# The feed-forward layers of two token chunks by Strassen's algorithm: seven block products in place of eight

## The chip, the cores and the metric

One core of a Trainium2 chip runs the whole program. The engines are TensorE (PE in the rows, its weight load PEld), VectorE (DVE), ScalarE (ACT), GpSimd (POOL) and SyncE (SP), which only issues transfers here. The metric is the device time of one execution in microseconds (us); the time before is 3068.78 us, the median of three runs (3066.46 to 3073.22).

## What is computed

One layer of a decoder: a projection, three groups of heads (mLSTM, RWKV-7, differential attention), an output projection with a residual, and a feed-forward layer with a residual; then a final norm. SEQ is 2048, D_MODEL 1024, D_FF 4096, all in float32. What the change touches is the end:

```
x = x + concat(A, B, C) @ w_out
x = x + relu(RMSNorm(x) @ w_ff_up)^2 @ w_ff_down
out = RMSNorm(x) * final_g
```

## The kernel before

The sequence is cut in four chunks of T = 512 tokens, features on the 128 partitions. After the heads, class `Tail` handles a chunk: `load` brings the mixed heads of the chunk in from DRAM and splits each of 8 tiles into a high and a low part, `outproj` multiplies by w_out and adds the residual (tiles `x2`, 8 per chunk), `hidden` is the norm and splits the result (`hh`, `hl`), `ffn` is the feed-forward layer, `final` the last norm and the store.

Every float32 product is made of three matmuls (`mm3`): high by high, high by low, low by high, each of a 128x128 weight tile against 512 tokens. `Weights.get` loads a unit of weights in four parts and splits each: ACT writes the high part `whi`, POOL subtracts for the low part `wlo` (lines 174 and 175, `split`). There are six buffers each of `whi` and `wlo`.

Chunks 0 and 1 go through `ffn` one after the other; chunks 2 and 3 go through it together (two `items`), so each unit of weights serves both: 16 steps `fb`, in each `up(fb)` with 96 matmuls and `down(fb)` with 96, for the two chunks. `down` adds its product to `x2` in place, on DVE (line 1176). Chunk 2 has a set of pools of its own (`tr`), chunk 3 has those of `tl`; the tile `nacc`, in which `norm` sums the squares and then keeps the scale that it multiplies by, is there once in each set.

The text order around chunk 3 is: with step 16 of chunk 1's `ffn` come `outproj(3)` and `hidden(x3)`, then the last `down` of chunk 1, then the `ffn` of chunks 2 and 3, and within its first step `final(1, x1)`. The order in each engine's queue is made from the text by a list scheduler, which takes priorities from the text order (`high_priority` puts a block first); where two tiles share a buffer, the one that is first in the text has it first.

Of the kernel before, what the change touches and what calls it, by code (L numbers as in the profile page):

```python
# [40 lines left out]
def load(nc, i, out, in_):  # L41
    (nc.sync if i % 2 == 0 else nc.scalar).dma_start(out, in_)
# [6 lines left out]
class Lane:  # L49


    def __init__(s, tc, p):
        s.tc, s.p = tc, p
# [91 lines left out]
    nc.tensor.matmul(ps, e.ones, dg, start=True, stop=True)  # L145


def norm(tc, e, sp, raw, pp, ptag, src, gofs, emit, w=T):
# [20 lines left out]
    for k in range(KT):  # L169
# [49 lines left out]
class Proj:  # L219
# [855 lines left out]
class Tail:  # L1075


    def __init__(s, ctx, tc, e, xt, wo, wu, wd, out, nh, nx, nr=3, w=None):
        s.tc, s.e, s.xt, s.wo, s.wu, s.wd, s.out = tc, e, xt, wo, wu, wd, out
        p = lambda n, **k: ctx.enter_context(tc.tile_pool(name=n, **k))  # L1080
        s.nr = nr
        s.hp = p("th", bufs=nh)
        s.xp = p("tx", bufs=nx)
        s.w = w or Weights(tc, e, p("tw", bufs=2))
        s.ap = p("ta", bufs=2)
        s.np = p("tn", bufs=2)
        s.pd = p("pdt", bufs=2, space=PSUM)
        s.py = p("pyt", bufs=2, space=PSUM)

    def hl(s):  # L1090
        return (s.hp.tile([P, T], F32R, name="hh", tag="hh"), s.hp.tile([P, T], F32R, name="hl", tag="hl"))

    def raw(s):
        return s.np.tile([P, T], F32, name="traw", tag="traw", bufs=s.nr)

    def load(s, c):

        nc = s.tc.nc
        m = []
        for k in range(KT):  # L1100
            r = s.raw()
            load(nc, k, r, s.e.mixT[c][k * P:(k + 1) * P])
            t = s.hl()
            split(nc, t[0], t[1], r, nc.vector)
            m.append(t)
        return m

    def outproj(s, c, m, x2, xp):
        nc = s.tc.nc
        for u in range(4):  # L1110
            w = s.w.get(s.wo[u], 256)
            for j in range(2):
                d = 2 * u + j
                xr = s.raw()
                load(nc, d, xr, s.xt[c, d])
                ps = s.pd.tile([P, T], F32, name="pd", tag="pd")
                mm3(nc, ps, [(*w(k, j * P, (j + 1) * P), m[k][0], m[k][1]) for k in range(KT)])
                t = xp.tile([P, T], F32, name="x2", tag="x2")
                with s.tc.high_priority():
                    nc.vector.tensor_tensor(t, ps, xr, ALU.add)  # L1120
                x2.append(t)
            yield u

# [13 lines left out]
            norm(s.tc, s.e, s.np, s.raw, s.pd, "pd", x2, V_N2, emit)  # L1137
        return h2

    def ffn(s, items):  # L1140

        tc, nc = s.tc, s.tc.nc
        FB = 16
        acts = {}

        def up(fb):
            w = s.w.get(s.wu[fb], 256)
            acts[fb] = []
            for tl, x2, h2 in items:
                ah = tl.ap.tile([P, 2, T], F32R, name="ah", tag="ah")  # L1150
                al = tl.ap.tile([P, 2, T], F32R, name="al", tag="al")
                for j in range(2):
                    ps = tl.pd.tile([P, T], F32, name="pd", tag="pd")
                    mm3(nc, ps, [(*w(k, j * P, (j + 1) * P), h2[k][0], h2[k][1]) for k in range(KT)])
                    with tc.high_priority():
                        r = tl.raw()
                        nc.scalar.activation(r, ps, AF.Relu)
                        nc.scalar.activation(r, r, AF.Square)
                        split(nc, ah[:, j], al[:, j], r, nc.vector)
                acts[fb].append((ah, al))  # L1160

        def down(fb):
            w = s.w.get(s.wd[fb], 1024, kt=2)
            av = acts.pop(fb)
            last = fb == FB - 1
            parts = [(d, i) for d in range(KT) for i in range(len(items))]
            if last:

                parts.sort(key=lambda x: x[1])
            for d, i in parts:  # L1170
                tl, x2, h2 = items[i]
                ah, al = av[i]
                ps = (s if last else tl).py.tile([P, T], F32, name="py", tag="py")
                mm3(nc, ps, [(*w(j, d * P, (d + 1) * P), ah[:, j], al[:, j]) for j in range(2)])
                with tc.high_priority():
                    nc.vector.tensor_tensor(x2[d], ps, x2[d], ALU.add)  # L1176

        up(0)
        yield 0
        for fb in range(1, FB):  # L1180
            up(fb)
            yield fb
            down(fb - 1)
        yield FB
        down(FB - 1)
# [14 lines left out]
            norm(s.tc, s.e, s.np, s.raw, s.pd, "pd", x2, V_FG, emit)  # L1200


@with_exitstack
def tile_hybrid_layer(ctx: ExitStack, tc: tile.TileContext, xt, wi, wg, wm, wo, wu, wd, vf, vg, lw, hb, tb, lq, cm, out, dbg=None, upto=9):
    nc = tc.nc
    e = Env()
# [4 lines left out]
    def scr(name, shape):  # L1211
        return e.dp.tile(shape, F32, name=name)
# [40 lines left out]
    xs = {}  # L1253
# [45 lines left out]
    if upto < 3:  # L1299
        actx.close()  # L1300
        return
    tl = Tail(ctx, tc, e, xt, wo, wu, wd, out, nh=10, nx=17)
    x0, x1, x2, x3 = [], [], [], []
    for _ in tl.outproj(0, tl.load(0), x0, tl.xp):
        pass
    h0 = tl.hidden(x0)
    for fb in tl.ffn([(tl, x0, h0)]):
        if fb == 15:
            m1 = tl.load(1)
        if fb == 16:  # L1310
# [90 lines left out]
```

## Time and profile before

| | us |
|---|---|
| median of three runs | 3068.78 |
| the profiled execution's own time | 3073.17 |
| its span in the trace | 3071.4 |
| feed-forward of chunks 2 and 3, last `down` of chunk 1 ahead of it, to the last matmul | about 2315 to 3045 |
| from the last such matmul to the end | about 26 |

The profiled execution is 4.4 us above the median. A row of the stage view gives for a stretch how long each engine was busy, how many instructions it ran (x), and the granted TensorE clock (PEclk: 1.00 is 2.4 GHz, 0.50 is 1.2 GHz). A matmul's own duration in the rows is longer than its turn, since matmuls overlap: the turn is read from how many run in a stretch. In the timeline a row's bracket says how long its engine was idle before it and what ended that.

### The profile page before, as it was taken

What the parts mean: (1) busy time and instruction counts of PE and PEld (TensorE: products, weight loads), DVE (VectorE), ACT (ScalarE), POOL (GpSimd) and SP (SyncE); (2) the same over time, 40 slices, a digit from 0 to 9 for tenths busy, and PEclk for the clock granted to TensorE, in tenths of its full rate; (3) what the DMA queues carried; (4) which work ended last, traced back from release to release, by engine and by line L of the source; (5) the groups of instructions that cost most, each with busy time, mean ns of one, the idle gap of its engine ahead of it and who ended that gap; (6) DMA issues with size and microseconds to landing.
All of it is one profiled execution on the core that took longest, in us unless ns stands there. A gap on an engine that the chain in (4) does not pass through costs nothing.

```text
span 3071.4 us, 47398 instructions
## 1 busy us (share of the span) xinstructions
PE 2959.1 (96%) x17232; PEld 2431.0 (79%) x17232; DVE 1719.6 (56%) x4055; ACT 1201.4 (39%) x2389; POOL 1090.1 (35%) x1047
## 2 busy tenths in 40 slices
PE   9999999999999889999999999999999999999997
PEld 7886787778878767888888788888787888888885
DVE  6587878677773456554555765554365333333335
ACT  5343334223322445544545555444344223222323
POOL 4354444333433214433333433433454222222223
PEclk9999999999999889999999999999999999999998
DMA  8445333643543554444446343332452111111111
GB/s 307 128 135 198 88 92 84 214 117 92 149 150 115 158 147 109 110 121 109 115 107 170 101 128 104 109 103 76 131 154 81 53 49 48 42 54 50 48 42 66
DMA packets 285348, 342.03 MB, mean 111 GB/s; under 512 B 99349, under 2 KB 161078, under 8 KB 284090
## 3 DMA queue, kind: packets, MB, share of 16 engines
q1 hardware_dynamic: 203914, 233.46, 26.3%
q10 hardware_dynamic: 81200, 105.53, 12.1%
q8 instruction: 136, 2.23, 0.3%
q14 instruction: 98, 0.80, 0.1%
HBM read 264.68 MB, written 74.21 MB: 110 GB/s over the span
## 4 chain that ended last, share of the span: by engine, by line
PE 63%; DMA 3%; DVE 2%; POOL 1%; SPq 1%; ACT 0%; issue 0%; DVEq 0%; ACTq 0%; POOLq 0%
PE pd L182 10%; PE pd L183 10%; PE pd L184 10%; PE py L182 8%; PE py L183 7%; PE py L184 7%; PE pO L1056 4%; PE pS L1026 2%; PE pS L1027 2%; PE pT L1051 2%; DMA Qd<-aql 1%; DMA traw<-mixT 0%; POOL x L1194 0%; PE nps L145 0%; DMA Qd<-aqh 0%
## 5 line engine op out<-in xcount | busy, mean ns | idle before, releaser
L175 POOL TENSOR_TENSOR wlo<-wraw,whi 128x512 fp32r<-128x512 f32 (+2 forms) x560 | 765.7, 1380 | 1322.9 <-ACT whi L174 885.1
L174 ACT ACTIVATE whi<-wraw 128x512 fp32r<-128x512 f32 (+2 forms) x560 | 347.1, 626 | 660.8 <-PE py L183 370.6
L1176 DVE TENSOR_TENSOR x<-py,x 128x512 f32<-128x512 f32 x512 | 350.1, 689 | 443.0 <-PE py L184 440.6
L182 PE MATMUL pd<-hh,whi 128*128 128x512 f32 x1280 | 504.3, 397 | 4.3 <-ACT hh L174 4.3
L183 PE MATMUL pd<-hl,whi 128*128 128x512 f32 x1280 | 504.4, 395 | 1.1 <-DVE hl L175 1.1
L184 PE MATMUL pd<-hh,wlo 128*128 128x512 f32 x1280 | 501.5, 395 | 0.0
L182 PE MATMUL py<-ah,whi 128*128 128x512 f32 x1024 | 405.0, 398 | 0.7 <-ACT whi L174 0.5
L183 PE MATMUL py<-al,whi 128*128 128x512 f32 x1024 | 400.4, 394 | 0.6 <-DVE al L175 0.6
L184 PE MATMUL py<-ah,wlo 128*128 128x512 f32 x1024 | 399.0, 394 | 1.2 <-POOL wlo L175 1.2
L182 PEld LDWEIGHTS pd<-hh,whi 128*128 128x128 f32 x1280 | 241.5, 189 | 58.1 <-ACT hh L174 5.6
L183 PEld LDWEIGHTS pd<-hl,whi 128*128 128x128 f32 x1280 | 242.0, 189 | 55.1 <-DVE hl L175 2.5
L184 PEld LDWEIGHTS pd<-hh,wlo 128*128 128x128 f32 x1280 | 241.8, 189 | 52.5 <-issue 0.2
L1030 DVE TENSOR_SCALAR_CACHE_REDUCE E<-pS 128x512 f32<-128x512 f32 (+4 forms) x320 | 185.9, 607 | 152.2 <-PE pS L1027 95.3
L175 DVE TENSOR_TENSOR al<-traw,ah 128x512 fp32r<-128x512 f32 x128 | 113.6, 888 | 215.8 <-ACT ah L174 215.1
L182 PE MATMUL pd<-hhi,whi 128*128 128x512 f32 x544 | 224.5, 416 | 7.6 <-ACT hhi L279 6.5
L184 PEld LDWEIGHTS py<-ah,wlo 128*128 128x128 f32 x1024 | 192.2, 188 | 44.7 <-POOL wlo L175 1.6
L182 PEld LDWEIGHTS py<-ah,whi 128*128 128x128 f32 x1024 | 192.6, 188 | 43.4 <-ACT whi L174 1.1
L183 PEld LDWEIGHTS py<-al,whi 128*128 128x128 f32 x1024 | 192.5, 188 | 42.4 <-DVE al L175 0.8
L184 PE MATMUL pd<-hhi,wlo 128*128 128x512 f32 x544 | 225.4, 417 | 0.0
L183 PE MATMUL pd<-hlo,whi 128*128 128x512 f32 x544 | 224.3, 414 | 0.4 <-POOL hlo L175 0.3
L1037 ACT ACTIVATE E<-E,nm 128x128 f32<-128x128 f32 (+15 forms) x128 | 153.7, 1201 | 99.2 <-DVE nm L1033 81.9
L182 PE MATMUL pd<-whi,hhi 128*128 128x256 f32 (+1 forms) x640 | 188.5, 295 | 2.5 <-DVE evx L408 1.2
(370 smaller groups left out, 5105.1 us busy)
## 6 DMA issues: line engine op xcount, KB each, us to landing
wraw<-in_wu ACTq DMA_DIRECT2D x96, 256.0 KB, 3.2
wraw<-in_wu SPq DMA_DIRECT2D x96, 256.0 KB, 3.2
wraw<-in_wd ACTq DMA_DIRECT2D x96, 256.0 KB, 3.2
wraw<-in_wd SPq DMA_DIRECT2D x96, 256.0 KB, 3.1
wraw<-in_wi ACTq DMA_DIRECT2D x48, 256.0 KB, 3.6
wraw<-in_wi SPq DMA_DIRECT2D x48, 256.0 KB, 3.6
feat<-hhi SPq DMA_DIRECT2D x4, 2048.0 KB, 9.5
feat<-hlo SPq DMA_DIRECT2D x4, 2048.0 KB, 12.4
```

What stands on the lines that cost most here:

```text
L174: nc.scalar.activation(hi, src, AF.Copy)
L175: lo_eng.tensor_tensor(lo, src, hi.bitcast(F32), ALU.subtract)
L182: nc.tensor.matmul(out, sh, mh, start=(i == 0), stop=False)
L183: nc.tensor.matmul(out, sh, ml, start=False, stop=False)
L184: nc.tensor.matmul(out, sl, mh, start=False, stop=(i == n - 1))
L1026: PE.matmul(s_[:, :k1 - k0], Q[c][0][:, qs], Kst[c][:, k0:k1], start=True, stop=False)
L1027: PE.matmul(s_[:, :k1 - k0], Q[c][1][:, qs], Kst[c][:, k0:k1], start=False, stop=not last)
L1030: V.tensor_scalar(E[:, k0:k0 + w], s_[:, :w], 0.125, None, ALU.mult, ALU.max, accum_out=mb[:, j:j + 1])
L1037: A.activation(E[:, :n], E[:, :n], AF.Exp, bias=nm, accum_out=l)
L1051: PE.transpose(t_[:, b * P:(b + 1) * P], Es[0][:, j * T + b * P:j * T + (b + 1) * P], e.ident)
L1056: PE.matmul(o[:, 0:P], pt[:, b * P:(b + 1) * P], vt[:, kb], start=(kb == 0), stop=(kb == i))
L1176: nc.vector.tensor_tensor(x2[d], ps, x2[d], ALU.add)
```

## The change

The feed-forward of chunks 2 and 3 becomes two matrix products in blocks of two by two: weights by halves of features in and out, activations by halves of features and by the two chunks. `Wino` makes each with seven block products on sums of blocks, in Winograd's form of Strassen's algorithm. 3072 matmuls of 128x512 become 2688, and it needs sums:

- of weights: `factors` loads four blocks and makes four sums of 128x1024 (on DVE in `up`, on POOL in `down`); each of the seven factors is then split by `unit`, ACT and POOL as before. There are 112 units of 128x512 in `up` and 112 in `down`, where 128 were split before for both.
- of activations for `up`: `first` norms chunk 2 and splits its 8 tiles, `second` norms chunk 3, makes the sums of both and splits them (20 pairs).
- of results: `up` adds parts of the seven products (`c1`, `u2`, `u3`), squares, and writes each of 64 tiles to DRAM (`e.act`). `down` runs in four stages `st`; in each it loads 16 tiles, makes 16 sums on DVE, splits 28 tiles (ACT and DVE) and adds seven products of four tiles each into `acc`; in the last stage POOL adds `acc` tiles into one another (28 adds, lines 1408 and 1410), and `final` follows.

The residuals of chunks 2 and 3 wait in DRAM (`e.x2d`). Chunk 2 no longer has pools of its own; `tl.np`, with `nacc` and the three `traw` buffers, serves both chunks. The end of the text order is now: `first` for chunk 2, the load of chunk 3's heads and `outproj(3)`, the last `down` of chunk 1, `final(1, x1)`, `second`, `up`, `down`.

```diff
-    for fb in tl.ffn([(tr, x2, h2), (tl, x3, h3)]):
-        if fb == 0:
-            tl.final(1, x1, (2, 5))
-    tr.final(2, x2, range(8))
-    tl.final(3, x3, (2, 4, 7))
+    tl.final(1, x1, (2, 5))
+    tl.actx.close()
+    tp = tl.hctx.enter_context(tc.tile_pool(name="tp", bufs=4))
+    wn.second(x2, x3, tp)
+    wn.up()
+    tl.hctx.close()
+    rctx.close()
+    wr2 = ctx.enter_context(tc.tile_pool(name="wr2", bufs=1))
+    ap = ctx.enter_context(tc.tile_pool(name="acc", bufs=1))
+    with tc.using_default_side("right"):
+        ar = ctx.enter_context(tc.tile_pool(name="au", bufs=5))
+    wn.down(ap, ar, wr2)
...
+    def second(s, x2, x3, tp):
...
+            s.rms(x3)
+            b11, b21, b12, b22 = x2[:4], x2[4:], x3[:4], x3[4:]
+            t2, t3, t1, t4 = [], [], [], []
+            for k in range(4):
+                G.tensor_tensor(b12[k], b22[k], b12[k], ALU.subtract)
+                V.tensor_tensor(b11[k], b12[k], b11[k], ALU.add)
+                t2 += s.cut(b11[k:k + 1], [tl.hl()], (V,))
...
+            for p in range(7):
+                b = (0, 0, 1, 1, 2, 1, 2)[p]
...
+                    for k in range(4):
+                        s.prod(o, w[q][0][:, k * P:(k + 1) * P], w[q][1][:, k * P:(k + 1) * P], s.ops[p][k], new and k == 0)
+                    m = 2 * fb + q
+                    with tc.high_priority():
+                        if p == 0:
+                            c1[q] = tl.slot(0)
+                            A.copy(c1[q], o)
...
+                        w = s.unit(ws[k // 2][:, k % 2 * T:k % 2 * T + T], G, 0)
+                        b = (ar.tile([P, T], F32R, name="uh", tag="uh"), ar.tile([P, T], F32R, name="ul", tag="ul"))
+                        split(nc, b[0], b[1], xs[k], V)
...
+                        if last:
+
+                            for i in {1: (0,), 2: (0,), 3: (2,), 5: (3,), 6: (2, 4)}.get(p, ()):
+                                G.tensor_tensor(a, a, acc[i][q], ALU.add)
+                            if p == 4:
+                                G.tensor_tensor(x22[q], x22[q], acc[3][q], ALU.add)
+                        V.tensor_tensor(a, ps[q], a, ALU.add)
```

Three places show how instructions move. The first is PE's queue where chunk 1 ends. Before, the norm of chunk 3 (`nps` tile 24601) stands among chunk 1's last `down` (`py`), with the new `up` (`pd`) around it:

```order
L184 MATMUL pd_24779<-hh_24080,wlo_24761 128x512 [waits Pool_49]
L162 MATMUL nps_24601<-ones_68,nacc_24578 128x1 [waits DVE_49]
L162 MATMUL nps_24601<-ones_68,nacc_24578 128x1 x3
L182 MATMUL py_24705<-ah_23801,whi_24666 128x512 [waits DVE_49]
L183 MATMUL py_24705<-al_23802,whi_24666 128x512
```

Now two norms stand one behind the other, after the last `down` and after product 0 of `up` (`py_24980`); tile `nacc_24751` is `final(1, x1)`, `nacc_24812` is the norm of chunk 3, and `pd_25052` is product 2, whose operands come out of `second`:

```order
L1221 MATMUL py_24980<-hh_24165,wlo_24962 128x512
L162 MATMUL nps_24774<-ones_68,nacc_24751 128x1 [waits DVE_49]
L162 MATMUL nps_24774<-ones_68,nacc_24751 128x1 x3
L145 MATMUL nps_24785<-traw_24786,ones_68 128x512 [waits DVE_49]
L162 MATMUL nps_24835<-ones_68,nacc_24812 128x1 [waits DVE_49,PE_49]
L162 MATMUL nps_24835<-ones_68,nacc_24812 128x1 x3
L145 MATMUL nps_24846<-traw_24847,ones_68 128x512 [waits DVE_49,Activation_49]
L1219 MATMUL pd_25052<-hh_24861,whi_25044 128x512 [waits Activation_49]
```

The norms moved behind all of the work that stood around them, and product 1 comes after product 2.

The second place is DVE's queue there now: the last of `final(1)`'s multiplies (line 1194), the sums of squares of chunk 3 in the same buffer `nacc` (159), and then the first of the multiplies of chunk 3 (1227):

```order
L1194 SCALAR_TENSOR_TENSOR x_20837<-x_20837,vf_58,nacc_24751 128x512
L1194 SCALAR_TENSOR_TENSOR x_20866<-x_20866,vf_58,nacc_24751 128x512
L159 TENSOR_TENSOR nacc_24812<-nacc_24812,traw_24814 128x512 [waits Activation_49,Pool_49]
L159 TENSOR_TENSOR nacc_24812<-nacc_24812,traw_24817 128x512 [waits DVE_49]
...
L159 TENSOR_TENSOR nacc_24812<-nacc_24812,traw_24832 128x512 [waits DVE_49,Activation_49]
L164 TENSOR_SCALAR nsm_24840<-nps_24835 128x4 [waits PE_49]
```

Before, the sums of chunk 3's norm came first, and `final(1)` after the new `up` had begun.

The third place is POOL's queue in the last stage of `down`: splits of weights (`wlo`), sums of weights (`wr`, 128x1024) and sums of `acc`:

```order
L175 TENSOR_TENSOR wlo_29868<-wr_29657,whi_29867 128x512 [waits PE_49,Activation_49]
L1408 TENSOR_TENSOR acc_27323<-acc_27323,acc_27319 128x512 [waits DVE_49]
L1408 TENSOR_TENSOR x_27335<-x_27335,acc_27319 128x512
L1289 TENSOR_TENSOR wr_29664<-wr_29668,wr_29431 128x1024 [waits Pool_49]
L175 TENSOR_TENSOR wlo_29888<-wr_29657,whi_29887 128x512 [waits PE_49,Activation_49]
L1408 TENSOR_TENSOR acc_27324<-acc_27324,acc_27320 128x512 [waits DVE_49]
```

Before, POOL's queue has only splits there; now the sums stand between the splits of one product and those of the next.

## Rows read from the trace of the kernel before

**Rows 1.** The page: busy time and share by engine, clock in 40 slices.

```profile
PE 2959.1 (96%) x17232; PEld 2431.0 (79%) x17232; DVE 1719.6 (56%) x4055; ACT 1201.4 (39%) x2389; POOL 1090.1 (35%) x1047
...
PEclk9999999999999889999999999999999999999998
```

**Rows 2.** Stages: busy us (x instructions) by engine, clock, DMA share, GB/s.

```profile
2262.00:2318.00 56.00, 56.00 (x251) 46.06 (x250) 38.04 (x43) 23.35 (x39) 34.93 (x25) 1.00 0.42 116
...
2340.00:2400.00 60.00, 57.34 (x239) 45.87 (x239) 29.88 (x41) 23.59 (x41) 20.58 (x15) 0.94 0.28 88
...
2400.00:2500.00 100.00, 100.00 (x433) 81.07 (x433) 32.89 (x46) 27.50 (x45) 23.72 (x18) 1.00 0.17 48
...
2900.00:3000.00 100.00, 100.00 (x435) 81.30 (x434) 30.85 (x42) 29.44 (x49) 25.21 (x19) 1.00 0.16 45
...
3050.00:3071.40 21.40, 2.84 (x9) 1.18 (x9) 7.86 (x10) 0.58 (x1) 11.22 (x9) 0.52 0.46 171
```

**Rows 3.** Groups by line, 2400 to 3000: xcount, busy us, mean ns, idle before.

```profile
L175 POOL TENSOR_TENSOR wlo<-wraw,whi 128x512 fp32r<-128x512 f32 x109 | 144.3, 1340 | 459.9 <-ACT whi L174 324.7 <-PE py L183 134.4
...
L1176 DVE TENSOR_TENSOR x<-py,x 128x512 f32<-128x512 f32 x213 | 145.9, 690 | 233.5 <-PE py L184 233.5
...
L175 DVE TENSOR_TENSOR al<-traw,ah 128x512 fp32r<-128x512 f32 x55 | 48.2, 877 | 171.6 <-ACT ah L174 171.0
...
L174 ACT ACTIVATE whi<-wraw 128x512 fp32r<-128x512 f32 x109 | 68.8, 631 | 328.4 <-PE py L183 289.5 <-DMA wraw<-in_wu 24.4 <-PE pd L183 12.9
```

**Rows 4.** Timeline at chunk 1's final norm: start, us, engine, line, instructions.

```profile
2362.02 0.95 PE L162 MATMUL nps<-ones,nacc 128*128 128x1 f32 x8
...
2365.63 2.07 PE L145 MATMUL nps<-traw,ones 128*128 128x512 f32 x2 [2.66 <-DVE traw L144]
...
2367.74 0.59 ACT L168 COPY nacc<-nps 128x512 f32<-128x512 f32 x1 [6.38 <-PE nps L145]
...
2368.35 0.63 PE L184 MATMUL pd<-hh,wlo 128*128 128x512 f32 x1
...
2368.36 6.21 DVE L1196 SCALAR_TENSOR_TENSOR x<-x,vf,nacc 128x512 f32<-128x512 f32 x6 [2.79 <-ACT nacc L168]
...
2368.78 0.63 PE L182 MATMUL pd<-hh,whi 128*128 128x512 f32 x1
```

**Rows 5.** Timeline of DVE: one add of the sum of squares.

```profile
2353.10 0.69 DVE L159 TENSOR_TENSOR nacc<-nacc,traw 128x512 f32<-128x512 f32 x1
```

**Rows 6.** Groups of DVE, 2329 to 2345.5, chunk 3's norm and split.

```profile
L1131 DVE SCALAR_TENSOR_TENSOR traw<-x,vf,nacc 128x512 f32<-128x512 f32 x8 | 7.6, 1001 | 1.7 <-ACT nacc L168 1.7
...
L175 DVE TENSOR_TENSOR hl<-traw,hh 128x512 fp32r<-128x512 f32 x4 | 5.4, 1357 | 0.0
```

**Rows 7.** Timeline, POOL and DVE both at work on SBUF tiles.

```profile
2281.62 3.35 POOL L175 TENSOR_TENSOR wlo<-wraw,whi 128x512 fp32r<-128x512 f32 x2
...
2282.15 3.37 DVE L1131 SCALAR_TENSOR_TENSOR traw<-x,vf,nacc 128x512 f32<-128x512 f32 x2
```

**Rows 8.** Stage view, a stretch in the attention of chunk 2.

```profile
1040.00:1060.00 20.00, 14.49 (x54) 9.43 (x53) 13.61 (x47) 10.05 (x28) 9.10 (x7) 0.68 0.65 170
```

**Rows 9.** POOL: a low part by min, median and max ns; a 256-wide group.

```profile
L175 POOL TENSOR_TENSOR wlo<-wraw,whi x109: 1288/1296/1643, 2406.8 to 2998.8; 128x512 fp32r<-128x512 f32 x109
...
L782 POOL TENSOR_TENSOR rY<-rY,rgt 128x256 f32<-128x256 f32 x16 | 12.6, 790 | 0.6
```

**Rows 10.** Timeline of the end: scale copied, multiplies, next norm.

```profile
3044.27 0.59 ACT L168 COPY nacc<-nps 128x512 f32<-128x512 f32 x1 [0.42 <-PE nps L145]
...
3044.93 10.73 POOL L1194 TENSOR_TENSOR x<-x,nacc 128x512 f32<-128x512 f32 x8 [4.95 <-ACT nacc L168]
...
3049.71 1.05 PE L162 MATMUL nps<-ones,nacc 128*128 128x1 f32 x8 [4.09 <-DVE nacc L159]
...
3060.11 0.58 ACT L168 COPY nacc<-nps 128x512 f32<-128x512 f32 x1 [11.07 <-PE nps L145]
```

**Rows 11.** The page: transfers of weight parts, KB each, us to landing.

```profile
wraw<-in_wu ACTq DMA_DIRECT2D x96, 256.0 KB, 3.2
```

More of the change, by code (lines that the diff above doesn't have):

```diff
@@ L145, in bcast_rows, with norm @@
     nc.tensor.matmul(ps, e.ones, dg, start=True, stop=True)
-def norm(tc, e, sp, raw, pp, ptag, src, gofs, emit, w=T):
+def norm(tc, e, sp, raw, pp, ptag, src, gofs, emit, w=T, order=range(KT)):
     nc = tc.nc
@@ L168, in norm @@
     nc.scalar.copy(acc, ps)
-    for k in range(KT):
+    for k in order:
         emit(k, src[k], e.vf[:, gofs + k:gofs + k + 1], acc)
@@ L1106, in load, with outproj @@
         return m
-    def outproj(s, c, m, x2, xp):
+    def outproj(s, c, m, x2, g, pd=None, keep=None):
         nc = s.tc.nc
@@ L1115, in outproj @@
                 load(nc, d, xr, s.xt[c, d])
-                ps = s.pd.tile([P, T], F32, name="pd", tag="pd")
+                ps = (pd or s.pd).tile([P, T], F32, name="pd", tag="pd")
                 mm3(nc, ps, [(*w(k, j * P, (j + 1) * P), m[k][0], m[k][1]) for k in range(KT)])
-                t = xp.tile([P, T], F32, name="x2", tag="x2")
+                t = s.slot(g[d // 4])
                 with s.tc.high_priority():
                     nc.vector.tensor_tensor(t, ps, xr, ALU.add)
+                    if keep:
+                        nc.sync.dma_start(keep[d], t)
                 x2.append(t)
@@ L1147, in up @@
             w = s.w.get(s.wu[fb], 256)
[L1148 to L1160, printed above, removed]
+            ah = s.ap.tile([P, 2, T], F32R, name="ah", tag="ah")
+            al = s.ap.tile([P, 2, T], F32R, name="al", tag="al")
+            for j in range(2):
+                ps = s.pd.tile([P, T], F32, name="pd", tag="pd")
+                mm3(nc, ps, [(*w(k, j * P, (j + 1) * P), h2[k][0], h2[k][1]) for k in range(KT)])
+                with tc.high_priority():
+                    r = s.raw()
+                    nc.scalar.activation(r, ps, AF.Relu)
+                    nc.scalar.activation(r, r, AF.Square)
+                    split(nc, ah[:, j], al[:, j], r, nc.vector)
+            acts[fb] = (ah, al)
         def down(fb):
             w = s.w.get(s.wd[fb], 1024, kt=2)
[L1164 to L1173, printed above, removed]
+            ah, al = acts.pop(fb)
+            for d in range(KT):
+                ps = s.py.tile([P, T], F32, name="py", tag="py")
                 mm3(nc, ps, [(*w(j, d * P, (d + 1) * P), ah[:, j], al[:, j]) for j in range(2)])
@@ L1225, in tile_hybrid_layer @@
     e.av = [scr(f"av{h}", [HALF, 512]) for h in range(2)]
+    e.act = [[scr(f"act{c}_{m}", [P, T]) for m in range(FF // P)] for c in range(2)]
+    e.x2d = [[scr(f"x2d{c}_{d}", [P, T]) for d in range(KT)] for c in range(2)]
     e.mixT = [scr(f"mixT{c}", [D, T]) for c in range(4)]
@@ L1301, in tile_hybrid_layer @@
         return
-    tl = Tail(ctx, tc, e, xt, wo, wu, wd, out, nh=10, nx=17)
+    tl = Tail(ctx, tc, e, xt, wo, wu, wd, out)
     x0, x1, x2, x3 = [], [], [], []
-    for _ in tl.outproj(0, tl.load(0), x0, tl.xp):
+    for _ in tl.outproj(0, tl.load(0), x0, (0, 1)):
         pass
     h0 = tl.hidden(x0)
-    for fb in tl.ffn([(tl, x0, h0)]):
+    for fb in tl.ffn(x0, h0):
         if fb == 15:
@@ L1310, in tile_hybrid_layer @@
         if fb == 16:
-            for _ in tl.outproj(1, m1, x1, tl.xp):
+            for _ in tl.outproj(1, m1, x1, (2, 3)):
                 pass
             h1 = tl.hidden(x1)
-    for fb in tl.ffn([(tl, x1, h1)]):
+    rctx = ExitStack()
+    for fb in tl.ffn(x1, h1):
         if fb == 0:
@@ L1319, in tile_hybrid_layer @@
             with tc.using_default_side("right"):
-                tr = Tail(ctx, tc, e, xt, wo, wu, wd, out, nh=8, nx=8, nr=2, w=tl.w)
-            op = tr.outproj(2, tr.load(2), x2, tr.xp)
+                pq = [ctx.enter_context(tc.tile_pool(name=f"pq{i}", bufs=2, space=PSUM)) for i in range(2)]
+                wr = ctx.enter_context(tc.tile_pool(name="wr", bufs=1))
+                tl.xp2 = ctx.enter_context(tc.tile_pool(name="tx2", bufs=1))
+                hp2 = rctx.enter_context(tc.tile_pool(name="th2", bufs=8))
+            op = tl.outproj(2, tl.load(2, hp2), x2, (0, 1), pq[0], e.x2d[0])
         if 12 < fb < 15:
@@ L1325, in tile_hybrid_layer @@
             list(op)
-            h2 = tr.hidden(x2)
+            wn = Wino(tl, wr, pq)
+            wn.first(x2, hp2)
             m3 = tl.load(3)
         if fb == 16:
-            for _ in tl.outproj(3, m3, x3, tl.xp):
+            for _ in tl.outproj(3, m3, x3, (4, 5), None, e.x2d[1]):
                 pass
-            h3 = tl.hidden(x3)
-    for fb in tl.ffn([(tr, x2, h2), (tl, x3, h3)]):
-        if fb == 0:
-            tl.final(1, x1, (2, 5))
-    tr.final(2, x2, range(8))
-    tl.final(3, x3, (2, 4, 7))
+    tl.final(1, x1, (2, 5))
[10 more added lines that the diff above has]
+    wn.down(ap, ar, wr2)
 def layout(inputs):
```

200 lines of the change are left out of this document (184 added, 16 removed).

## The prediction

> **What bounds the kernel now.** I first read the busy shares on the page, then stages, then the groups of the stage that changes. PE is busy 96% at nearly full clock [rows 1]. In the feed-forward of chunks 2 and 3 a stretch of 100 us holds 433 to 435 matmuls, PE is never idle and the clock is 1.00, so a matmul's turn is 100/434 = 0.2304 us [rows 2]. In the same stage the other engines wait for PE: the low parts of weights behind `whi`, which waits for PE to free a buffer, the adds behind `py` [rows 3]. Less matmul work is therefore worth its full time there, for as long as nothing else becomes late. Ahead of it the `down` of chunk 1 and chunk 3's projection also run without a gap (251 matmuls in 56 us), and the one hole is 2340 to 2400: 239 matmuls in place of 260, ten of them the norm's own, so 260 - 229 = 31 turns or 7.2 us are lost at the norm of `final(1)` [rows 2].
>
> **The change, part by part.** The profiled execution took 3073.2 us (span 3071.4); I add to that and take off 4.4 for the median.
>
> *Matmuls.* 384 fewer at 0.2304: **-88.5**.
>
> *Chunk 3's heads.* Their three raw tiles are now shared with `first`, and their splits on DVE stand behind the eight multiplies of chunk 2's norm. Before, this stretch had no gap [rows 2]. Now the first two tiles of `outproj(3)` may wait for operands one by one: eight DVE operations of 0.7 to 1.0 plus a norm of some 6, less what is loaded ahead, at most 12. I take the middle, **+7** (0 to 12).
>
> *The end of chunk 1.* This is the largest loss I see. `final(1)` and the norm of chunk 3 use the one `nacc`, so chunk 3's squares start only when `final(1)` has multiplied. Of the new `up`, only product 0 (24 matmuls) is ready. Product 1 waits for the copy of product 0 into a slot of `x2` that the last subtraction of `second` frees, and so stands behind product 2, which needs `second`. PE thus waits for a chain that starts near the end of product 0:
> - the norm from its first matmul to the scale's copy, 2362.0 to 2368.3: 6.3; then the six multiplies of DVE, 6.2 [rows 4];
> - a square and seven adds of 0.69 [rows 5]: 5.4;
> - some 3 where two weight sums of DVE and a split of POOL stand in the chain;
> - the second norm: 7, as 6.3 and a little for the lower clock;
> - 17 DVE operations to the fourth pair of product 2 (eight multiplies, four sums, five low parts). In chunk 3's norm before they took 1.00 and 1.36, with POOL busy beside them [rows 6]; alone such an operation is 0.69 [rows 5]. POOL's six weight buffers are full during the wait, but it has subtractions of the chain itself, so I take 0.9: 15.3.
>
> That is 6.3 + 6.2 + 5.4 + 3 + 7 + 15.3 = 43.2, less product 2's own 24 turns (5.5), through which it could have flowed: 37.7. Then product 1's sums and splits wait again: eight DVE operations (7.2) against 2.8 of work, +4.4. After the hole of before PE ran at half clock (turns of 0.42) for some 12 matmuls, 2.3 lost [rows 4]; I take +3. From 45 the 7.2 lost before come off: **+38**. With 0.69 an operation the gross is 43.2 - 3.6 - 2.1 (the multiplies at 0.69) - 2 - 5.5 + 2.7 + 3 = 36, net 28. Where POOL and DVE are both at work without rest, two of either take 3.35 and 3.37, 1.69 each [rows 7]; then 17 and 8 operations add 13 and 6: net 57.
>
> *Earlier parts.* Other pools move a few matmuls of chunk 0's projection in the attention of chunk 2, where PE waits for other engines anyway (14.5 busy of 20, clock 0.68 [rows 8]): **0** (-4 to 4).
>
> *`up`.* One step is 168 matmuls, 38.7 us. POOL splits 14 units (14 x 1.34 = 19 [rows 3]), DVE has four sums and some ten adds, ACT some 20 us. All are hidden; I take **+1** (0 to 5) for a late sum of weights, and **+2** (0 to 8) for the turn from `up` to `down`, where tiles come back from DRAM.
>
> *`down`, stages 0 to 2.* A stage is 336 matmuls: 77.4 us. POOL has 28 splits of 1.29 and eight sums of 128x1024. A 256-wide operation takes 0.79 and a 512-wide 1.29 [rows 9], so a 1024-wide is estimated at 1.29 + 2 x 0.5 = 2.29: 36.1 + 18.3 = 54.4. DVE has 44 operations with two inputs in SBUF (28 low parts, 16 sums). Beside one of these a POOL operation takes 1.68 in place of 1.29 [rows 7], so each may cost POOL 0.39: 54.4 + 17.2 = 71.6, 93% of the stage. It just fits; queue order will spoil some of it: **+4** (0 to 21).
>
> *`down`, last stage.* POOL has 19 splits, 27 sums and four wide sums behind product 0: 46 x 1.29 + 4 x 2.29 = 68.5, and PE needs the last split when six products less a quarter are done, 63.6 us on. POOL starts 1.2 earlier, so alone it is some 4 late; with 42 DVE operations at 0.39 it is 20 late. Not all of them meet: **+14** (0 to 32).
>
> *The end.* From the scale's copy of `final(2)` to the end were 26.5 us (3044.9 to 3071.4). There the norm of `final(3)` already ran beside POOL's eight multiplies of 10.7 [rows 10]. With one `nacc` it follows them: 10.8 + 0.6 + some 5 for the sum of squares + 7 + 10.7 (3060.7 to 3071.4) = 34.7, +8. The last 12 matmuls wait for a bank that `final(2)`'s norm holds, some 2 to 3 more: **+10** (6 to 13).
>
> Weight parts land in 3.2 us [rows 11] against steps of 38.7; they stay hidden.
>
> Sum: -88.5 + 7 + 38 + 1 + 2 + 4 + 14 + 10 = -12.5: 3060.7 on the profiled execution, **3056** on the median.
>
> The Trainium skill has a rule against this change ("SBUF — State Buffer", section "Who interferes with whom"): a DVE instruction with two SBUF inputs contends with a GpSimd one that reads SBUF, and whichever comes first holds the shared ports for its whole length while the other is fully blocked. Taken literally, each pair would take the sum of both; the pairs of the trace took 1.68, less than 0.69 + 1.29 = 1.98, so the trace agrees that they hinder one another, not that the exclusion is whole. By the trace the sum is 3056, by the rule it is rival B's.
>
> **The rivals.**
> - *A: POOL and DVE hardly meet in `down`.* POOL has 23 us free in a stage and its splits run ahead by six buffers, which speaks for it; the last stage, with 27 more sums, speaks against. Stages 0 to 2 then cost 0 and the last 4: 14 less, **3042**.
> - *C: the chain at the end of chunk 1 runs undisturbed.* POOL runs out of weight buffers, which speaks for it; its subtractions within the chain speak against. Net 28: **3046**; with A, 3032.
> - *B, slower: POOL and DVE exclude one another.* A joint stage is then 54.4 + 44 x 0.69 = 84.8, more than PE's 77.4. Three stages lose 22 in place of 4, the last some 32 in place of 14: **3092**. It decides from where POOL's time and its hindrance pass 77.4, thus at (77.4 - 54.4)/44 = 0.52 us for each DVE operation; rows show 0.39. Queues that alternate without slack would do the same.
> - *That it does not do what it says* is excluded: PE's order has 2688 matmuls in these products.
>
> **How the numbers follow.** Forecast's case 0.41, A 0.14, C 0.14, A with C 0.04, B 0.27. About 0.2% (6 us) is what a measurement of this kernel can tell from no change. The forecast's own terms move it between 3040 and 3073. Faster takes A, C, both, and 0.23 of the 0.41, so 0.55; same takes 0.13 of it and 0.05 where B is half so strong or meets C: 0.18; slower takes the rest of B and 0.05 of the forecast's case: 0.27. The range is 3030 to 3095: from A with C to B with a little beyond.
>
> **What would show it.** A matmul's turn stays at 0.230 in `up`. Ahead of the first `pd` of product 2 PE is idle for some 35 to 40 us in two or three pieces, ended by DVE and ACT, and the first matmuls behind it are 0.42 apart. Stages 0 to 2 of `down` last 77 to 79; in the last one PE waits for `wlo` and POOL is nearly full. From the scale's copy of `final(2)` to the end are some 34 us. I am wrong if PE waits at the end of chunk 1 for under 25 us, or if stages 0 to 2 take over 80: then a POOL operation there is longer than 1.7.

## The result, and the profile after

The changed kernel takes 3110.8 us (median of four runs, 3101.9 to 3121.2) against 3070.9 for the kernel before (four runs): a ratio of 1.0133, with a 95% interval of 1.0098 to 1.0168. It is 40 us slower. The forecast was 3056 and the upper end of its range 3095: it was wrong in direction and in size. The profiled execution took 3101.9 us, 9 under the median, so its rows show a difference of 28.8 us to the profiled execution of before.

The page of the changed kernel, busy times and clock, as in [rows 1]:

```profile
PE 2893.9 (93%) x16848; PEld 2365.7 (76%) x16848; DVE 1911.5 (62%) x4141; ACT 1299.1 (42%) x2577; POOL 1391.0 (45%) x1213
...
PEclk9999999999999899999999999999996999999997
```

The 384 matmuls are gone, and PE is busy 65 us less. Yet its share fell from 96% to 93%, in a longer span. DVE and POOL are busy 192 and 301 us more, with 86 and 166 instructions more: 2.2 and 1.8 us for each of these. Stages show where PE stands still. The first row is the boundary behind chunk 1, the others are stages 0 to 3 of `down` (columns as in [rows 2]):

```profile
2300.00:2400.00 100.00, 58.26 (x216) 43.70 (x215) 64.15 (x72) 33.72 (x59) 52.04 (x36) 0.74 0.18 60
2693.00:2790.60 97.60, 83.33 (x337) 65.84 (x336) 65.90 (x52) 43.41 (x80) 70.49 (x39) 0.93 0.51 168
2790.60:2876.80 86.20, 81.92 (x337) 63.75 (x336) 78.76 (x74) 32.12 (x58) 66.28 (x39) 0.98 0.32 98
2876.80:2959.50 82.70, 80.15 (x337) 62.73 (x336) 74.59 (x73) 31.42 (x56) 64.02 (x37) 1.00 0.32 96
2959.50:3069.30 109.80, 91.18 (x348) 69.38 (x346) 92.03 (x85) 39.98 (x68) 97.05 (x61) 0.91 0.01 2
```

A stage's 336 matmuls are 77.4 us of work. The four stages take 97.8, 86.3, 82.7 and 109.8 from their first matmul to that of the next (the last one to its last matmul). DVE is busy 75 to 79 us in each of stages 1 and 2, where 72 operations at 0.69 would be some 50. What PE waited for, from product 0 of `up` to the end (total us, times, longest):

```profile
PE nps L162 <- DVE nacc L159: 28.6, 3, 15.2
PE pd L1220 <- DVE ul L175: 18.9, 12, 4.0
PE nps L145 <- DVE traw L144: 12.7, 4, 4.6
PE pd L1219 <- ACT hh L174: 10.4, 1, 10.4
PE pd L1219 <- ACT whi L174: 9.1, 1, 9.1
PE pd L1221 <- POOL wlo L175: 5.7, 3, 3.8
PE py L1219 <- ACT x L1331: 4.4, 1, 4.4
PE pd L1220 <- DVE hl L175: 3.8, 2, 3.1
PE py L1221 <- POOL wlo L175: 2.2, 1, 2.2
```

`ul`, the low part of an activation in `down`, which DVE makes, was late twelve times. POOL's `wlo`, on which the forecast had laid its account of `down`, was late four times, three of them in the last stage. DVE's and POOL's groups in stage 1 (2790.6 to 2876.8) say why:

```profile
L175 DVE TENSOR_TENSOR ul<-x,uh 128x512 fp32r<-128x512 f32 x29 | 39.1, 1355 | 5.2 <-ACT uh L174 5.2
L1411 DVE TENSOR_TENSOR acc<-pd,acc 128x512 f32<-128x512 f32 x18 | 11.7, 677 | 1.1 <-PE pd L1221 1.1
...
L1376 DVE TENSOR_TENSOR x<-x 128x512 f32<-128x512 f32 x4 | 6.9, 1725 | 0.1
...
L175 POOL TENSOR_TENSOR wlo<-wr,whi 128x512 fp32r<-128x512 f32 x31 | 48.0, 1565 | 19.1 <-ACT whi L174 19.1
L1290 POOL TENSOR_TENSOR wr<-wr 128x1024 f32<-128x1024 f32 x2 | 5.7, 2841 | 0.0
```

An operation of DVE with both inputs in SBUF takes 1.25 to 1.75 us there, as the mean of its line (1.36 for `ul`); the add with one input in PSUM (line 1411), of the same size and in the same stage, takes 0.68. Piece by piece it is seen in the timeline of stage 0, first DVE's, then POOL's:

```profile
2734.91 1.77 DVE L175 TENSOR_TENSOR ul<-x,uh 128x512 fp32r<-128x512 f32 x1
2736.71 2.77 DVE L1373 TENSOR_TENSOR x<-x 128x512 f32<-128x512 f32 x1
2739.52 1.67 DVE L1376 TENSOR_TENSOR x<-x 128x512 f32<-128x512 f32 x1
2741.11 0.68 DVE L175 TENSOR_TENSOR ul<-x,uh 128x512 fp32r<-128x512 f32 x1
```

```profile
2734.40 1.73 POOL L175 TENSOR_TENSOR wlo<-wr,whi 128x512 fp32r<-128x512 f32 x1
2736.09 2.84 POOL L1290 TENSOR_TENSOR wr<-wr 128x1024 f32<-128x1024 f32 x1
2738.89 1.75 POOL L175 TENSOR_TENSOR wlo<-wr,whi 128x512 fp32r<-128x512 f32 x1
2742.36 1.30 POOL L175 TENSOR_TENSOR wlo<-wr,whi 128x512 fp32r<-128x512 f32 x1 [1.73 <-ACT whi L174]
```

The two go in step: a DVE operation that alone takes 0.68 (2741.11, POOL idle) lasts 1.7 beside a POOL operation of 512 columns and 2.8 beside one of 1024. POOL itself loses 0.4 (1.73 for 1.30). So a meeting costs POOL 0.4 and DVE 1.0 to 2.1. Not every operation of POOL meets one of DVE: over stage 1, DVE's operations on SBUF tiles take 33 us more than at 0.69 each, for 37 operations of POOL, 0.9 a piece.

The boundary, matmuls of the norms, of product 2 and the first of product 1 on PE, each with its wait, and DVE's eight multiplies of chunk 3:

```profile
2336.51 0.95 PE L162 MATMUL nps<-ones,nacc 128*128 128x1 f32 x8
...
2342.07 2.08 PE L145 MATMUL nps<-traw,ones 128*128 128x512 f32 x2 [4.62 <-DVE traw L144]
...
2359.34 1.84 PE L162 MATMUL nps<-ones,nacc 128*128 128x1 f32 x8 [15.19 <-DVE nacc L159]
...
2363.92 2.04 PE L145 MATMUL nps<-traw,ones 128*128 128x512 f32 x2 [2.74 <-DVE traw L144]
...
2376.34 1.22 PE L1219 MATMUL pd<-hh,whi 128*128 128x512 f32 x2 [10.38 <-ACT hh L174]
...
2388.09 0.50 PE L1220 MATMUL pd<-hl,whi 128*128 128x512 f32 x1 [0.63 <-DVE hl L175]
...
2393.73 0.79 PE L1219 MATMUL py<-hh,whi 128*128 128x512 f32 x1 [4.44 <-ACT x L1331]
```

```profile
2366.62 8.41 DVE L1227 SCALAR_TENSOR_TENSOR x<-x,vf,nacc 128x512 f32<-128x512 f32 x8 [2.85 <-ACT nacc L168]
```

This is the chain of the forecast, link by link: norm of `final(1)`, its multiplies and chunk 3's squares (15.2), second norm, multiplies and sums (10.4), then product 1 behind the copy of product 0 (4.4). The first step of `up` takes 92.9 us from its first matmul (2330.9) to the last (2423.8), where its 168 matmuls are 38.7. At the end the order is also the one forecast: ACT's copy of `final(2)`'s scale, and the first square of `final(3)`, which waits for POOL's multiplies in `nacc`:

```profile
3066.01 0.57 ACT L168 COPY nacc<-nps 128x512 f32<-128x512 f32 x1
...
3076.54 0.63 ACT L155 ACTIVATE nacc<-x 128x512 f32<-128x512 f32 x1 [9.96 <-POOL acc L1192]
```

From the end of that copy (3066.6) to the end (3100.2) are 33.6 us, where before there were 26.5 [rows 2, 10].

How to compare profiles of this program: the order of instructions up to `up` is the same in the changed kernel and in six of the experiments, yet `up` began between 2330.9 and 2354.5 us. The parts behind it repeat far better: the first step of `up` takes 92.5 to 93.0 wherever it is not edited, steps 2 to 8 take 269.2 in all of them, stage 1 as the change left it 85.2 to 86.3. Stage 0 does not repeat so well: as the change left it, it took 97.8 here, and 98.0 and 104.3 in two of the runs below. So a change of 5 us is read below from its stage, in stage 0 only with care; the medians, which contain the early part too, confirm only the larger ones.

### The profile page after: what moved, and what is told of

Read it like the earlier page. It is cut to its first block, busy times and chain, and to the rows that moved or that the text cites. A ratio compares the mean times of both kernels' runs of the same rounds, so it can differ in the third digit from the quotient of the medians.

```text
span 3100.2 us, 47371 instructions
## 1 busy us (share of the span) xinstructions
PE 2893.9 (93%) x16848; PEld 2365.7 (76%) x16848; DVE 1911.5 (62%) x4141; ACT 1299.1 (42%) x2577; POOL 1391.0 (45%) x1213
## 3 DMA queue, kind: packets, MB, share of 16 engines
q10 hardware_dynamic: 84400, 116.02, 12.6%
## 5 line engine op out<-in xcount | busy, mean ns | idle before, releaser
L175 POOL TENSOR_TENSOR wlo<-wr,whi 128x512 fp32r<-128x512 f32 x224 | 325.0, 1461 | 222.2 <-ACT whi L174 194.3
L183 PE MATMUL pd<-hl,whi 128*128 128x512 f32 x768 | 304.5, 397 | 6.9 <-DVE hl L175 6.9
L182 PE MATMUL pd<-hh,whi 128*128 128x512 f32 x768 | 302.3, 398 | 5.8 <-ACT hh L174 5.3
L184 PE MATMUL pd<-hh,wlo 128*128 128x512 f32 x768 | 301.2, 396 | 0.1
L1174 DVE TENSOR_TENSOR x<-py,x 128x512 f32<-128x512 f32 x256 | 174.8, 688 | 197.2 <-PE py L184 196.1
L1030 DVE TENSOR_SCALAR_CACHE_REDUCE E<-pS 128x512 f32<-128x512 f32 (+4 forms) x320 | 185.6, 607 | 147.9 <-PE pS L1027 88.5
L182 PE MATMUL py<-ah,whi 128*128 128x512 f32 x512 | 207.0, 405 | 1.2 <-DVE x L1174 0.6
L183 PE MATMUL py<-al,whi 128*128 128x512 f32 x512 | 203.2, 397 | 0.4 <-DVE al L175 0.4
L184 PE MATMUL py<-ah,wlo 128*128 128x512 f32 x512 | 201.6, 397 | 0.0
L183 PE MATMUL pd<-wlo,hhi 128*128 128x256 f32 (+1 forms) x640 | 186.9, 292 | 0.0
L184 PE MATMUL pd<-whi,hlo 128*128 128x256 f32 (+1 forms) x640 | 185.7, 290 | 0.0
```

The costliest lines, as they stand in the source:

```text
L1030: V.tensor_scalar(E[:, k0:k0 + w], s_[:, :w], 0.125, None, ALU.mult, ALU.max, accum_out=mb[:, j:j + 1])
```

## The experiments

**The norm of chunk 3 ahead.** 

```diff
+            with tc.high_priority():      # fb == 16, behind outproj(3)
+                wn.rms(x3)
...
-            s.rms(x3)                     # in second
```

> The changed kernel with one move: the norm of chunk 3 (squares, scale and its eight multiplies, in place) stands in the text right behind outproj(3), ahead of the last down of chunk 1 and of final(1), as in the kernel before. Theory (the chain through the one nacc makes the boundary): the squares, the second norm and the eight multiplies, 5.5 + 7 + 10 = 22 us, leave the chain between product 0 and product 2 of up, part of it comes back because product 1 still waits for the slots that final(1) frees; the stretch from the first matmul of product 0 to the end of the first step of up falls from 92.9 us to 68 to 78, the time by 15 to 25 (3086 to 3096 against 3111). Rival (DVE has too many operations there whatever their order): the work is the same, the stretch stays over 86 and the time within 8 of 3111.

Measured: 3104.5 us. The first step of `up` takes 85.3, down by 7.6, not by 15 to 25: the theory held for the squares' wait (15.2, gone) but not for the whole. The step lies between the two forecasts and the time is within the rival's 8. The wait moved: product 0 waits 6.2 in its middle, until ACT has made the first square of `final(1)` in `nacc`, which now comes behind chunk 3's multiplies; product 1 waits 10.2 for the copy of product 0, whose slot `second` frees late, and product 4 waits 5.9 for its operands. One link taken out uncovers the next, here `second`'s own operations on DVE.

**The weight sums of `down` on DVE.**

```diff
-            f = [s.factors(..., G)
+            f = [s.factors(..., V)
```

> The changed kernel with the weight sums of down (8 of 128x1024 a stage) on DVE in place of POOL. Theory (an operation of DVE with both inputs in SBUF lasts as long as the POOL operation that runs beside it): in stages 1 and 2 eight operations of DVE no longer take 2.8 but 0.7 to 1.7, some 12 to 17 us less, and DVE gets 8 x 1.22 = 10 more, so the stages fall from 86.2 and 82.7 to 78 to 82 and the time by 8 to 20. Rival (DVE simply has too many operations, or its sums stand ahead of its splits): 10 us more of work on DVE make each stage 4 to 10 longer, 3125 to 3150.

Measured: 3089.7 us (ten runs). Stages 91, 80.0, 81.7 and 101 in place of 98, 86, 83 and 110. DVE got eight more operations a stage and was faster: `ul` in stage 1 fell from 1.36 to 1.08 us, since there are no POOL operations of 2.8 left beside it. The rival had the opposite sign. What is left of POOL's work there, 27 splits in stage 1, still costs DVE 20 us, 0.7 a piece.

```profile
L175 DVE TENSOR_TENSOR ul<-x,uh 128x512 fp32r<-128x512 f32 x28 | 29.8, 1079 | 4.1 <-ACT uh L174 4.1
```

**The low parts of the weights on DVE as well.**

```diff
-                        w = s.unit(..., G, 0)
+                        w = s.unit(..., V, 0)
```

> The changed kernel with the weight sums and the low parts of the weights of down all on DVE: POOL has nothing there but the 28 sums of the last stage. Theory (as for the run before: POOL at work costs DVE about 1.0 us an operation, while doing the same split itself costs DVE 0.69): DVE has 72 x 0.69 + 8 x 1.22 + 28 x 0.68 = 78.5 us of work a stage and nothing holds it, so stages 1 and 2 last 78 to 84 although DVE does everything and POOL nothing; the last stage stays near 100 to 110; the time is 3090 to 3115. Rival (too many operations on DVE): 29 us more a stage, stages of 105 to 115, the time over 3180.

Measured: 3080.0 us (ten runs), 31 less than the changed kernel and 10 under the theory's range. Stages 1 and 2, and DVE's groups in stage 1:

```profile
2798.50:2877.20 78.70, 78.70 (x338) 63.27 (x337) 69.89 (x109) 32.31 (x57) 0.00 (x0) 1.00 0.33 107
2877.20:2955.70 78.50, 78.50 (x337) 63.12 (x336) 69.78 (x108) 32.12 (x57) 0.00 (x0) 1.00 0.30 101
```

```profile
L175 DVE TENSOR_TENSOR wlo<-wr,whi 128x512 fp32r<-128x512 f32 x29 | 20.2, 698 | 10.3 <-ACT whi L174 10.3
L175 DVE TENSOR_TENSOR ul<-x,uh 128x512 fp32r<-128x512 f32 x28 | 19.5, 696 | 0.0
```

DVE does 109 instructions in place of 74 in 69.9 us in place of 78.8; POOL does none, and PE never stops. This decides between the theories: DVE was not short of time for its own work, it stood beside POOL's. Stage 0 falls to 91.0 and the last stage, where POOL keeps its 28 sums, to 99.7.

**The residuals loaded later.**

```diff
-            for p, c, d in ((1, 0, 0), (5, 0, 4), (6, 1, 0)):   # ahead of stage 0
...
+                if st == 0 and p < 3:                           # behind product p
+                    p_, c, d = ((1, 0, 0), (5, 0, 4), (6, 1, 0))[p]
```

> The changed kernel with the loads of 12 residual tiles (3 MB) at the turn from up to down put behind products 0 to 2 of stage 0, one group of four behind each, without priority. Theory (the turn waits for transfers: 12 MB move between 2681 and 2714 at 390 to 400 GB/s, and the weights of the second half land last): 3 MB less is 7.5 us less, the wait of 9.1 us of PE for whi falls to 0 to 3 and stage 0 from 97.8 to 86 to 92, the time by 6 to 10. Rival (the load waits for room that up frees): the wait stays at 7 to 9 and the time is unchanged.

Measured: 3107.9 us, within the spread of the changed kernel. What PE waited for in stage 0:

```profile
PE pd L1220 <- DVE ul L175: 9.5, 4, 3.9
PE pd L1219 <- ACT whi L174: 3.9, 1, 3.9
```

The wait for `whi` fell from 9.1 to 3.9, so the transfers did make it; but `ul` was waited for longer (9.5 for 5.1), and stage 0 lasts 100.2. Half the theory: the cause of that wait is right, while a gain is not shown. How much there is to gain can't be read from this run: stage 0 without the edit took 97.8, 98.0 and 104.3, and the slowest of these also waits 9.5 for `ul`. Nor did the burst get smaller: 12.1 MB move in the 40 us around the turn with the edit as without, only in another order.

**`second` on DVE alone.**

```diff
-                G.tensor_tensor(b12[k], b22[k], b12[k], ALU.subtract)
+                V.tensor_tensor(b12[k], b22[k], b12[k], ALU.subtract)
...
-                t3 += s.cut(b12[k:k + 1], [tl.hl()], (G, V))
+                t3 += s.cut(b12[k:k + 1], [tl.hl()], (V,))
```

(and so for the four other subtractions and the last cut)

> The changed kernel with the twelve operations that POOL has in second (eight subtractions of activations, four low parts) on DVE; nothing else. Theory (POOL at work on SBUF tiles costs DVE 1.0 us an operation, the operation itself costs DVE 0.69): from the scale's copy of chunk 3 the fourth pair of product 2 comes after 20 x 0.69 = 14 us in place of 21.5, the first step of up falls from 92.9 to 82 to 88, the time by 5 to 11 (3100 to 3106). Rival (DVE is the bound by its number of operations, POOL takes load off it): 12 x 0.69 = 8 more, the step lasts 96 to 101, the time 3114 to 3120.

Measured: 3106.7 us; the first step of `up` takes 85.2, down by 7.7, as the theory had it. DVE does twelve operations more and is done sooner. The time, 4 under the changed kernel's, is within the spread and does not show it by itself; in the profiled execution (3117.9) stage 0, which the edit does not touch, took 104.3.

**The sums of the last stage on DVE as well,** on top of the two edits of `down` above (lines 1408 and 1410, `G` to `V`).

> The kernel with the weight sums and low parts of down on DVE, and now the 28 sums of the last stage on DVE as well: POOL does nothing in down. Theory: these sums cost DVE 28 x 0.69 = 19 in place of 28 holds of 1.0, so the last stage falls from 99.6 to 91 to 96; the time from 3080 to 3071 to 3077. Rival (POOL unloads DVE in the last stage, where DVE is full): the stage grows by 10 to 19, the time is 3090 or more.

Measured: the last stage takes 93.5 in place of 99.7, as the theory had it. The median, 3084.8 (ten runs), does not show it: it lies 5 over that of the kernel without this edit. Some 3.5 of these 5 may be the chip's: the two were measured on different chips, where the kernel before took 3074.1 and 3070.6. As ratios to it they are 1.0029 (1.0009 to 1.0049) and 1.0033 (1.0014 to 1.0053), the same. Of the two profiled executions the one here (3091.7 us) began `up` at 2354.5, the other (3078.9) at 2336.4.

**Residuals later and the end mended,** on top of that.

```diff
+                tl.final(2, acc[1] + acc[5], (1, 3, 5, 7))
...
+        tl.final(3, acc[6] + x22, (2, 4, 7), acc[0][0])     # squares summed in a tile of acc
```

> The run before with two more edits: the 12 residual tiles are loaded behind products 0 to 2 of stage 0, and the end: final(3) sums its squares in a tile of acc that is free by then in place of nacc, and final(2) gives half of its multiplies to DVE. Theory: with POOL out of down the wait that took the place of the transfers' (low parts of activations) is gone, so stage 0 falls from 91 to 83 to 87; from the scale's copy of final(2) to the end 33.6 become 24 to 28; the time is 8 to 14 under that of the run before, 3059 to 3067. Rival (stage 0 is limited by something behind the transfers, such as the half clock; the end by the norm's own chain): stage 0 stays at 89 to 91, the end over 30, less than 5 gained.

Measured: 3060.8 us (ten runs), ratio to the kernel before 0.9960 (0.9937 to 0.9983). Stage 0 falls from 91.2 to 83.5, with 3.0 of waiting: without POOL's work beside it the later load is worth 7.7. With POOL out of `down`, stage 0 takes 83.5 to 85.4 in the four runs that load the residuals later, and 91.0 and 91.2 in the two that do not. The end missed its numbers: from the copy of the scale 31.2 us, not 24 to 28. `final(3)` no longer waits for `nacc` but for the last 12 matmuls, which still wait for `final(2)`'s norm to leave a PSUM buffer; from the last matmul's start to the end are 28.1 (30.9 in the changed kernel).

**All of it,** with the boundary mended: the norm of chunk 3 ahead, `second` on DVE, and

```diff
-                            c1[q] = tl.slot(0)
+                            c1[q] = tl.slot(0) if fb else tl.raw()
```

> The run before with the boundary mended: the norm of chunk 3 ahead of the last down of chunk 1, second on DVE alone, and the copies of product 0 in the first step of up in the raw tiles instead of slots that second frees, so that product 1 need not wait. Theory: the first step of up falls from 92.9 to 66 to 78 (38.7 are its matmuls), the time to 3035 to 3050, under the kernel before. Rival (the boundary is bound by DVE's operations for the twenty pairs whatever the order): 85 and 3050 to 3060.

Measured: 3052.9 us (seven runs), ratio 0.9941 (0.9918 to 0.9963). The first step of `up` takes 77.4, as the theory had it; the time lies 3 over its range. What PE waits for there now, the two longest:

```profile
PE nps L163 <- DVE nacc L160: 14.0, 1, 14.0
PE py L1220 <- ACT nacc L156: 4.1, 1, 4.1
```

The 14 us are again in front of a norm's matmuls, now those of `final(1)`, whose squares stand behind `second` in DVE's queue while PE's queue has them ahead of products 1 and 4.

**`first` on DVE alone,** on top of all:

> The run with all edits, and the low parts of first (chunk 2, eight, half of them on POOL) all on DVE. Theory (POOL's operation costs DVE 1.0, the own one 0.69): the eight low parts of chunk 3's heads behind them come up to 1 us sooner, the turns that PE loses from 2200 to the first matmul of up fall from 12 to 9 to 11; the time 3050 to 3053. Rival (these waits come from the loads of the heads in their three raw tiles): 12 to 14 lost, no gain.

Measured: 3049.7 us, ratio 0.9926 (0.9908 to 0.9945). From 2200 to the first matmul of `up` 13.5 us are lost, no less than the 12.6 without the edit: the rival's side, and the median's 3 us are within the spread.

**The heads of chunk 3 ahead of `first`,** on top of all:

```diff
+            m3 = tl.load(3)
             wn.first(x2, hp2)
-            m3 = tl.load(3)
```

> The run with all edits, and the load of chunk 3's heads ahead of first in the text, so that their splits have DVE first. Theory (the heads' splits behind eight multiplies of chunk 2 cost what I took for them, 7 or more): the loss from 2200 to the first matmul of up falls from 12 to 5 to 8, the time to 3045 to 3049. Rival (the norm of first then stands in PE's queue without other matmuls around it, and PE waits some 5 to 6 for its scale): the loss stays at 11 to 14.

Measured: 3062.2 us, ratio 0.9964 (0.9950 to 0.9978); 17.7 lost. PE waits 4.5 and 2.7 for the norm of `first`, now bare of other matmuls, as the rival said. The theory fell: the loss there is not only the order of those splits.

**The kernel before, with DVE in POOL's place** for the low parts of weights in the feed-forward of chunks 2 and 3:

> The kernel before, with the low parts of the weights in the feed-forward of chunks 2 and 3 on DVE in place of POOL. Theory (a hold costs time only where DVE has none to spare): DVE was busy a third of that stretch and PE 100%, so nothing changes, the turn stays at 0.2304, the time within 0.2% of the kernel before. Rival (POOL at work slows this stage too, or DVE's own splits come late): the stage from 2400 to 3000 holds over 2610 or under 2590 matmuls, the time moves by over 0.3%.

Measured: 3071.5 us (ten runs), ratio 0.9998 (0.9986 to 1.0010). The stretch from 2400 to 3000, before and with the edit, and one group in it:

```profile
2400.00:3000.00 600.00, 600.00 (x2596) 486.88 (x2596) 193.09 (x268) 166.86 (x274) 144.21 (x109) 1.00 0.17 47
2400.00:3000.00 600.00, 600.00 (x2597) 487.10 (x2596) 254.60 (x379) 169.21 (x278) 0.00 (x0) 1.00 0.17 48
```

```profile
L175 DVE TENSOR_TENSOR al<-traw,ah 128x512 fp32r<-128x512 f32 x56 | 38.7, 691 | 89.6 <-ACT ah L174 89.0
```

`al` fell from 0.88 [rows 3] to 0.69, PE ran 2597 matmuls in place of 2596, and the time did not change: where DVE has time to spare the meetings are free.

## Why the prediction was wrong

Term by term, forecast against measured, in us of the profiled executions: matmuls -88.5 and as forecast (steps 2 to 8 of `up` have a turn of 269.2/1176 = 0.229). Chunk 3's heads +7 against some 14 (2200 to 2330.9 holds 501 matmuls, which leaves 15.5, of them some 1.5 the norm's own; before none). The boundary +38 against 92.9 - 38.7 - 7.2 = +47. `up` +1 against -2. The turn and stages 0 to 2 +6 against 97.8 + 86.3 + 82.7 - 232.2 = +35. The last stage with its last 12 matmuls, +17, and the end, +7, against 109.8 - 77.4 = 32 and 5 from the last matmul's start, 37 together. That is +42, and the medians differ by 40. That the two agree so well is in part luck: the two profiled executions themselves differ by 28.8, since the one of the changed kernel was ahead before any of this began (its 13600th matmul starts at 2195.7, that of before at 2205.6; in the six runs with the same order up to there, between 2197.8 and 2219.4).

**The step that failed** is the account of `down`: "each may cost POOL 0.39: 54.4 + 17.2 = 71.6, 93% of the stage. It just fits". The price of a meeting was read from [rows 7], where both engines show 1.69, and charged to POOL alone. The same rows show what it costs DVE: 1.69 in place of 0.69, two and a half times as much as POOL loses, and beside the weight sums, which the trace of before did not have, 2.8. DVE's own account was never added up for `down`: 44 operations at 1.4 (what `ul` took) and 28 adds at 0.68 are 81, over the 77.4 of PE. Measured, DVE was busy 78.8 and 74.6 in stages 1 and 2, and its waits for ACT came on top. The forecast sought the bound on the wrong one of the two engines. Its sign of being wrong came true, stages of over 80, but not for the reason that it gave: POOL's splits took 1.57 in stage 1, less than 1.7. The kernels with POOL taken out of `down` show it: DVE does all, and stages 0 to 2 fall by 6.8, 7.6 and 4.0, to 91.0, 78.7 and 78.7, the last one with its sums by 16, to 93.5, some 34 us in all. Only in the last stage was the forecast's own account right in part: PE waited 7.3 there for `wlo`, beside 7.7 for `ul`.

Rival B came nearest (3092). It had the same meetings, priced as full exclusion, and put the wait on POOL; 22 for stages 0 to 2 were 35 with the turn, 32 for the last stage were 32. Its number is near in part by luck, since the waits were mostly for DVE. The rule from the Trainium skill ("SBUF — State Buffer", "Who interferes with whom") weighed there says that the loser is blocked for the whole of the other's instruction. On DVE's side this trace agrees: in the timeline of stage 0 each of the three held operations ends 0.55 us after the POOL operation beside it, whether that took 1.73 or 2.84, and alone it takes 0.68. On POOL's side it does not show a block of the whole length: 0.43 lost, not 0.68. That a DVE instruction with at most one SBUF input does not contend (outside the two-port modes), which the same section says, agrees too: 0.677 for the adds out of PSUM.

**The boundary** was right in its mechanism and its order; the chain's size was short by 9. Its mis-sized term is "17 DVE operations", of which it says "I take 0.9: 15.3": from the scale's copy (2366.6) to the wait that the fourth pair ends (2388.1) were 21.5, 1.26 each, by the same meetings with POOL's subtractions. The rows had it: at the 1.00 and 1.36 of [rows 6] the 17 are 20.2. The other 2.7 are the clock: behind the waits 27 matmuls of products 2 and 1 start mostly 0.43 apart in place of 0.23, 5.7 lost in place of 3 (granted clock 0.63 from 2376.3 to 2389.3 and 0.50, its lower level, from 2393.7 to 2399.5). The run with `second` on DVE gave 7.7 of it back. That it is a chain of several links, and not only `nacc`, is shown by the run with the norm ahead, which won 7.6 and met the next wait.

**The turn** from `up` to `down` was forecast at +2. The changed kernel waits 9.1 there for weights behind a burst of transfers from 2681 to 2714, some 358 GB/s on average (390 to 410 in its faster stretches, not all through), and the clock is lower (0.93 over the stage). The DMA view of 2680 to 2720 counts it:

```profile
DMA packets 6546, 12.09 MB, mean 302 GB/s; under 512 B 656, under 2 KB 656, under 8 KB 6544
```

A weight transfer of 512 KB lands in 7.7 to 8.2 us there, in 4.1 to 4.5 in `up`. The rows of before show no such burst (171 GB/s at most, [rows 2]); the activations' loads were counted, their bytes were not.

**The end** was right: 33.6 against 34.7 from the copy. **The heads** were forecast at half of what they cost, and two experiments did not find the rest. The rows of the changed kernel do. The wait that was forecast came with its size, 6.9 for a low part behind the eight multiplies; what the forecast had at nothing is a wait of 2.2 for the squares of `first` and, behind each of the two waits, a row of matmuls at the lower clock, 0.43 apart, which cost some 5 together (granted clock 0.57 from 2252 to 2260, 0.50 from 2276 to 2280):

```profile
2252.13 1.39 PE L162 MATMUL nps<-ones,nacc 128*128 128x1 f32 x8 [2.19 <-DVE nacc L159]
...
2263.80 8.46 DVE L1227 SCALAR_TENSOR_TENSOR x<-x,vf,nacc 128x512 f32<-128x512 f32 x8
...
2275.68 0.80 PE L183 MATMUL pd<-hl,whi 128*128 128x512 f32 x1 [6.92 <-DVE hl L175]
2276.27 0.63 PE L184 MATMUL pd<-hh,wlo 128*128 128x512 f32 x1
```

No run shows how to be rid of them: with the heads ahead the wait for the low part went and others came. It was not traced why the early part, with one order of instructions, ends up to 24 us apart from one execution to the next.

## What to carry to other kernels

Where DVE and POOL both work on tiles in SBUF, add up both engines with the longer durations that the trace shows for each when they meet; an operation handed to POOL cost DVE about as much as doing it (0.7 as a mean over a stage of `down`, against 0.69) or more (1.0 in `second`) as soon as DVE had no time to spare, and nothing while it had. A saving on the engine that bounds the kernel is worth its full size only in stages where the helpers have room: here 88 us of matmuls were bought with 130 of losses at seams, and with POOL out of `down` and `second` and the seams mended the same algorithm is 0.6 to 0.7% faster than the kernel before. Behind the waits read above PE also ran 9 to 14 matmuls at the lower clock, which belongs to a wait's price. After an edit look at the stage, not only at the sum: an edit that was right can show little until the next wait behind it is gone.

## What the runs showed of the hardware

The meeting is lopsided. In the changed kernel, beside one another, an operation of 128x512 took 1.73 on POOL (1.30 alone) and 1.77 on DVE (0.68 alone), one of 128x1024 took 2.84 on POOL and held a DVE operation of 512 columns for 2.77. The 128x1024 sum itself took 1.24 on DVE alone. DVE's add of a PSUM tile to an SBUF tile stayed at 0.68 through all of it.
